# Taps given out by counted work, and parts of VectorE's work moved to ScalarE and a DMA, in a hybrid attention and convolution layer

## The chip, the cores and the metric

The kernel runs on one core of one Trainium2 chip. The metric is the device time of one execution in microseconds (us). Before the change it is 491.62 us, the median of 3 runs (489.23 to 491.92). The engines are named as the profile names them: PE (TensorE, matmul), PEld (its weight loads), DVE (VectorE), ACT (ScalarE), POOL (GpSimd) and SP (SyncE, which issues all DMAs of the kernel before).

## The reference, cut to what matters

One encoder layer for 1024 prompt frames and 64 sample frames, with 16 meta tokens, 1104 tokens in all, of 1024 features in f32. One input projection feeds an attention group and a convolution group; each is normalised, gated and multiplied with its half of the output projection.

```python
q, k, v, ga, u, gb = _split(_rms(h_p, g_pre[l]) @ w_in[l])      # u = a * sigmoid(b)
att  = _prompt_attention(q, k, v, mk, mv, sinks[l])             # windows of 3 chunks of 64 keys + meta
conv = _conv_branch(u, left, conv_w[l], ln_g[l], ln_b[l], w_pw[l])
#   31 depthwise taps over u, LayerNorm over channels, silu, @ w_pw
y = concat([_rms(att, g_att) * silu(ga), _rms(conv, g_conv) * silu(gb)]) @ w_out
h_p = h_p + _rms(y, g_post)
```

The softmax is over the keys and a learned sink; its P is e / sum, and P multiplies v.

## The kernel before, in words

**Products in three parts.** A product of f32 accuracy is three products of rounded parts: high weights x high x, high weights x low x, low weights x high x. `hi_w` (L162) copies a raw weight tile of 128 x 1024 into its high part, mostly on ACT; `lo_w` (L174) subtracts that from the raw tile on DVE. `split_w` is both. A unit (`unit`, L301) is one weight tile times one of three token groups n (384, 384, and 336 or 320 columns): 8 k-slices x 3 parts = 24 matmuls. In the first group (n = 0) it takes all 16 matmuls with high weights first (`SK`), in the others slice by slice (`KS`). At a fixed point of a unit (`ahead`, L179) the weights of the next one are split: for the GLU's `a` weights (AT) at n = 0, for its `b` weights (BT) at n = 2, else at n = 1. `load_raw` puts the weight after that on SP's queue; the raw tiles have two buffers. `WORDER` (L44) is the order of the weights: AT, BT, AT+1, BT+1, KM (keys), AT+2, BT+2, VM (values), AT+3, BT+3, the four q tiles (QT), the gates, and two tiles of the pointwise weights.

**The start** (L681 to L765). x comes in three token groups. Group 0 is split without its norm; the norm's factor goes into the results of the first four units (`late`). Later `renorm` (L261) scales the tile of group 0 on DVE, and `resplit` (L266) splits it again on ACT and DVE. Groups 1 and 2 are squared row by row on ACT (`square_rows`), the sums become a factor (`stat_x`, DVE and POOL), which `diag_x` (DVE) and `bcast_x` (a matmul) spread, `scale_x` (DVE) multiplies, and `hi_x`, `lo_x` split. Lists `at={step: [...]}` say behind which matmul each such step is issued. a0, b0, a1, b1 are the units of the first two pairs of GLU weights; a0[0] and b0[0] are their units on group 0, run in turn, matmul by matmul.

**Order.** Instructions stay in program order on each engine (`keep_in_program_order`), so the place where the Python code issues something is its place in the queue.

**Taps.** When the GLU output u of one of four channel groups is complete, `conv` (L422) puts 31 taps into the list `taps`; each is one DVE instruction over 1118 columns of H. Behind every matmul of a unit, `tick` (L331) may issue one: it counts matmuls, and whenever the count reaches `pace` (9.2, 9.4, 10.0 or 7.5 in different parts), the next tap goes out.

**Attention** (L881 to L932). `order` has 17 chunks of 64 queries. One pass of the loop issues the scores of chunk i (`att_scores`: 12 matmuls, then a bias and a minimum on DVE into T), the high and low parts of the next queries (`att_prep`: ACT, DVE), the transposes of the chunk before (`att_transpose`; PSUM copies on ACT, in later chunks one of two on DVE), the exponentials of chunk i (ACT), their division by the sums (`norm`, L618: a reciprocal and four scalings on DVE), and the products with v of the chunk before (`att_values`). Between these, `fill` issues matmuls of the 24 gate units' queue. From pass L0 = 11 on, the taps that are left are issued at once, and the LayerNorm runs in steps (`ln_pre`, `ln_mean`, `ln_var`, `ln_diag`, `ln_scale`). Pass 17 also splits the last pointwise weights. Then come the pointwise products and the output projection.

Of the kernel before, what the change touches and what calls it, by code (L numbers as in the profile page):

```python
# [48 lines left out]
def layer_kernel(ctx: ExitStack, tc: tile.TileContext, x, x_fm, w_in, w_pw, w_out, vec, g_post,  # L49
# [13 lines left out]

    class Engine:


        def __init__(self, engine):
            self.engine = engine

        def __getattr__(self, name):  # L70
# [288 lines left out]
    def ab_units(i, seqs=(None,) * 3, bps=(("s", 2),) * 3):  # L359
# [48 lines left out]
        for n in range(3):  # L408
            out.append((unit(AT + i, n, done_a, seqs[n]), unit(BT + i, n, done_b, seqs[n], bps[n])))
# [229 lines left out]
    def att_transpose(c):  # L639
# [3 lines left out]
        for n, (end, v) in enumerate(avs.pop(c)):  # L643
# [4 lines left out]
            if n == 0 or c == NCHUNK or c < 8:  # L648
# [33 lines left out]
    for _ in range(11):  # L682
# [6 lines left out]
    load_raw(1, [h1])  # L689
# [29 lines left out]
    def by(u, m):  # L719
# [5 lines left out]
    HW_, LW = hi_w, lo_w  # L725
    hi_x(0, 0)
    hi_w(0, b=4)
    hi_w(1, True, b=4)
    lo_x(0, 0)
    run(a0[0], b0[0], at={  # L730
        0: [L(S, 0, 1), L(S, 0, 2), L(LW, 0, b=4), L(LW, 1, b=4)],
        6: [L(S, 0, 3), L(S, 0, 4), L(HW_, 0, a=4), L(HW_, 1, True, a=4), L(S, 0, 5)],
        9: [L(S, 0, 6), L(S, 0, 7), L(LW, 0, a=4), L(LW, 1, a=4), L(load_raw, 3, [h1, h2])]
        + [L(load_x, 1, g) for g in range(3)] + [L(load_rows, 0, 0)],
        16: [L(split_w, 2, dst=(wq[:, 0], wq[:, 1]), b=4), L(split_w, 2, a=4)]})
    run(a1[0], at={
        0: [L(Q, 1, 0), L(Q, 1, 1), L(split_w, 3, dst=(wq[:, 2], wq[:, 3]), b=4), L(split_w, 3, a=4), L(Q, 1, 2), L(load_rows, 0, 1, 2)] + [L(load_x, 2, g) for g in range(3)]
        + [L(load_rows, 2, 0)],
        18: [L(stat_x, 1)]})
    run(b1[0], at={  # L740
        0: [L(diag_x, 1)],
        12: [L(bcast_x, 1), L(N, 1, 0)] + [L(H_, 1, k) for k in range(3)],
        18: [L(L_, 1, k) for k in range(3)] + [L(Q, 0, 0), L(load_rows, 2, 1), L(N, 1, 1), L(Q, 0, 1), L(load_rows, 2, 2)]})
# [36 lines left out]
    def add_ab(i):  # L780
        pace[0] = 9.4
# [3 lines left out]
    def add_kv(mi, dst):  # L785
        pace[0] = 9.4
# [84 lines left out]
    pace[0] = 9.4  # L871
# [10 lines left out]
    pace[0] = 10.0  # L882
# [3 lines left out]
    fill(16)  # L886
    L0, GATE, REST = 11, (9, 11, 12, 14, 16), 72
    for i in range(max(len(order) + 1, L0 + 7)):
# [28 lines left out]
        if 0 < i <= len(order):  # L917
            att_values(order[i - 1])
        if 0 < i < len(order):
            att_v(order[i])  # L920
        if i == len(order):
# [254 lines left out]
```

## Time and profile before

| | us |
|---|---|
| time, median of 3 runs | 491.62 (489.23 to 491.92) |
| the profiled execution: its time, its span | 493.84, 492.0 |
| busy PE, PEld, DVE | 468.4, 422.7, 392.6 |
| busy ACT, POOL | 213.6, 83.4 |
| mean granted TensorE clock, as a share of full speed | 0.974 |

The span is from the first to the last instruction. Matmuls are pipelined and their ends are modelled, so a busy PE need not be at its peak; how many matmuls it gets through in a stretch says more. The stretches used below: 0 to 68 us the start, 68 to 196 the remaining units up to q, with taps, 196 to 362 attention with the gate units, then the pointwise products and the output projection. The busy time of an engine is a mean over these stages, and each has its own limit.

### The profile page before, as it was taken

The numbers are of one execution on the slowest core, as the hardware profiler recorded it, in microseconds if no ns is written. First come the engines' busy times: TensorE is split into PE (matmuls) and PEld (weight loads), VectorE is DVE, ScalarE is ACT, GpSimd is POOL, SyncE is SP. The second block draws the span as 40 slices with busy tenths as digits, with TensorE's granted clock in tenths as the row PEclk, the third lists the DMA queues.
The fourth block names the chain that finished last, engine by engine and source line by source line (L and its number), as shares of the span: only waits on it lengthen the run. The fifth ranks groups of instructions, "written<-read, shape, count | busy, mean of one in ns | idle before, by whom it ended". The sixth has DMA issues, their size and how long they took to land.

```text
span 492.0 us, 7351 instructions
## 1 busy us (share of the span) xinstructions
PE 468.4 (95%) x2801; PEld 422.7 (86%) x2801; DVE 392.6 (80%) x684; ACT 213.6 (43%) x500; POOL 83.4 (17%) x105
## 2 busy tenths in 40 slices
PE   7988979999999999899999987999999999999994
PEld 6968979999999999898888875888999887888884
DVE  3565789999999999999999997798587955654533
ACT  5565333024212122356666543656687434433322
POOL 0000100000000000000332133164464521011100
PEclk8999989999999999899999987999999999999998
DMA  8993011101202111110101010102113602322221
GB/s 286 338 357 110 0 29 62 45 30 59 65 5 86 43 44 43 44 43 7 47 7 45 7 47 3 50 24 69 44 52 120 213 27 86 103 85 87 85 106 66
DMA packets 14474, 37.76 MB, mean 77 GB/s; under 512 B 2376, under 2 KB 4664, under 8 KB 14440
## 3 DMA queue, kind: packets, MB, share of 16 engines
q1 hardware_dynamic: 14440, 37.31, 22.6%
q8 instruction: 22, 0.36, 0.3%
q14 instruction: 12, 0.10, 0.1%
HBM read 32.00 MB, written 4.84 MB: 75 GB/s over the span
## 4 chain that ended last, share of the span: by engine, by line
PE 52%; DVE 36%; ACT 4%; issue 3%; DMA 3%; SPq 1%; POOL 0%; DVEq 0%; POOLq 0%; ACTq 0%
PE g L81 23%; DVE H L74 20%; PE y L81 19%; DVE T L74 4%; PE pw L81 4%; ACT xT L74 3%; DVE wlo L74 3%; DVE xT L74 2%; DMA H<-in_x_dram 2%; PE s L81 2%; PE av L81 1%; DMA x<-in_x_fm_dram 1%; DVE x L74 1%; DVE qs L74 1%; DVE wo L74 1%
## 5 line engine op out<-in xcount | busy, mean ns | idle before, releaser
L81 PE MATMUL g<-xT,whi 128*128 128x384 f32 (+2 forms) x960 | 231.8, 341 | 4.1 <-ACT whi L74 2.7
L81 PEld LDWEIGHTS g<-xT,whi 128*128 128x128 f32 x960 | 171.1, 193 | 12.4 <-ACT whi L74 2.9
L74 DVE SCALAR_TENSOR_TENSOR H<-u,vec_t,H 128x1118 f32<-128x1118 f32 x120 | 166.6, 1388 | 2.5
L81 PE MATMUL g<-xT,wlo 128*128 128x384 f32 (+2 forms) x480 | 138.1, 334 | 0.0
L81 PEld LDWEIGHTS g<-xT,wlo 128*128 128x128 f32 x480 | 89.4, 190 | 2.2 <-issue 1.5
L81 PE MATMUL y<-wo,mh 128*128 128x512 f32 (+2 forms) x304 | 89.1, 381 | 0.2 <-DVE wo L74 0.2
L81 PEld LDWEIGHTS y<-wo,mh 128*128 128x128 f32 (+1 forms) x304 | 55.1, 185 | 12.1 <-DVE wo L74 0.6
L81 PE MATMUL y<-wo,ml 128*128 128x512 f32 (+1 forms) x136 | 51.2, 378 | 0.0
L74 POOL TENSOR_TENSOR asq<-asq 128x128 f32<-128x128 f32 (+2 forms) x18 | 17.4, 964 | 124.2 <-ACT asq L74 123.5
L74 DVE SCALAR_TENSOR_TENSOR y<-y,small,y 128x512 f32<-128x512 f32 (+1 forms) x19 | 13.7, 720 | 28.2 <-PE y L81 28.2
L74 ACT ACTIVATE T<-T,st 128x210 f32<-128x210 f32 (+2 forms) x68 | 30.4, 451 | 9.6 <-DVE st L74 9.6
L81 PEld LDWEIGHTS y<-wo,ml 128*128 128x128 f32 x136 | 25.6, 188 | 4.5
L74 ACT ACTIVATE yj<-y 128x512 f32<-128x512 f32 (+2 forms) x21 | 12.8, 608 | 30.7 <-DVE y L74 30.6
L74 DVE TENSOR_TENSOR wlo<-wraw,whi 128x1024 fp32r<-128x1024 f32 (+1 forms) x23 | 25.8, 1130 | 0.0
L81 PE MATMUL g<-xT,wq 128*128 128x384 f32 (+1 forms) x144 | 25.4, 333 | 0.0
L81 PEld LDWEIGHTS g<-xT,wq 128*128 128x128 f32 x144 | 24.2, 188 | 0.5
L74 ACT ACTIVATE whi<-wraw 128x1024 fp32r<-128x1024 f32 (+1 forms) x21 | 21.2, 1011 | 6.5 <-PE g L81 6.1
L74 ACT ACTIVATE PT<-pa 128x512 f32<-128x512 f32 (+2 forms) x17 | 10.1, 596 | 28.4 <-PE pa L84 28.4
L74 DVE CUSTOM_DVE_ANT_0 T<-s,bias 128x210 f32<-128x210 f32 (+2 forms) x68 | 20.6, 358 | 1.8 <-PE s L81 1.8
L74 ACT ACTIVATE qb<-g 128x384 f32<-128x384 f32 (+1 forms) x12 | 5.7, 475 | 36.5 <-PE g L81 36.5
L74 POOL MEMSET gb<- 128x30 f32 x4 | 1.6, 391 | 110.2 <-PE g L81 60.5
L74 ACT ACTIVATE y<-y,small 128x512 f32<-128x512 f32 (+1 forms) x19 | 12.6, 665 | 15.3 <-PE y L81 15.3
(195 smaller groups left out, 604.3 us busy)
## 6 DMA issues: line engine op xcount, KB each, us to landing
wraw<-in_w_in_dram SPq DMA_DIRECT2D x18, 512.0 KB, 3.4
H<-in_x_dram SPq DMA_DIRECT2D x8, 512.0 KB, 7.2
xr<-in_x_dram SPq DMA_DIRECT2D x8, 512.0 KB, 4.1
out_dram<-o SPq DMA_DIRECT2D x7, 512.0 KB, 2.9
woraw<-in_w_out_dram SPq DMA_DIRECT2D x6, 512.0 KB, 3.5
wraw<-in_w_in_dram SPq DMA_DIRECT2D x8, 256.0 KB, 5.5
x<-in_x_fm_dram SPq DMA_DIRECT2D x4, 384.0 KB, 6.3
x<-in_x_fm_dram SPq DMA_DIRECT2D x2, 576.0 KB, 6.9
```

What stands on the lines that cost most here:

```text
L74: ins = op(*a, **k)
L81: return tc.keep_in_program_order(nc.tensor.matmul(*a, **k))
```

## The change

It keeps a count of planned time per engine, `given`, in nanoseconds: each matmul adds its columns at 2.4 a nanosecond plus 14, at least 109 (half for 64 rows); each operation of ACT adds 200 + 0.82 per column, of DVE 60 + 1.18 per column, from PE's count on if that is further. `tick` issues taps while DVE's count is less than 600 ns ahead of PE's. `freer` answers "act" or "dve" and decides at three places. For weights from the fifth on, `lo_w` may copy the negated high part on ACT and have a DMA from POOL's queue add the raw weights to it. P's scalings may go to ACT, one by one. P's PSUM copies go to either. The products with v move from the end of a pass to behind the scores of the next one, and there is one pass more. The LayerNorm's first pass L0 is now found in the loop: from pass 9, when fewer than 2 taps are left, or pass 12. In the start, a0[0] runs alone and then b0[0], with b0's raw weights loaded behind x; `renorm` moves from the last part of the start to b1[1]'s matmuls; the split for KM moves one unit ahead.

```diff
+    given = dict(pe=0.0, dve=0.0, act=0.0)
...
                 ins = op(*a, **k)
+                if self.name:
+                    n = columns(k["out"] if "out" in k else a[0])
+                    given[self.name] = max(given[self.name], given["pe"]) + self.each * (1 + ("accum_out" in k)) + self.column * n
                 return keep(ins) if pinned[0] else ins
...
+    act, dve, pool = Engine(nc.scalar, "act", 200, 0.82), Engine(nc.vector, "dve", 60, 1.18), Engine(nc.gpsimd)
+    def freer():
+        return "act" if given["act"] < (given["pe"] + LATE if taps else given["dve"]) else "dve"
+    def mm(out, lhsT, rhs, **k):
+        n = columns(rhs) * (4 if rhs.dtype == F32 else 1) / 2.4
+        if lhsT.shape[0] == HD or out.shape[0] == HD:
+            n /= 2
+        given["pe"] += max(14 + n, 55 if lhsT.shape[0] == HD else 109)
+        return tc.keep_in_program_order(nc.tensor.matmul(out, lhsT=lhsT, rhs=rhs, **k))
...
     def lo_w(p, a=0, b=KT):
...
+        if p > 3 and freer() == "act":
+            act.activation(lo, hi.bitcast(F32), AF.Copy, scale=-1.0)
+            pool.dma_start(out=lo, in_=raw, accum_op=ALU.add)
+            return
         dve.tensor_tensor(out=lo, in0=raw, in1=hi.bitcast(F32), op=ALU.subtract)
...
+    FIRST = [(0, 0), (0, 1), (1, 0), (1, 1), (0, 2), (1, 2)] + [(k, s) for k in range(2, KT) for s in (0, 2, 1)]
+    SECOND = [(k, s) for m in (0, 4) for s in (0, 1, 2) for k in range(m, m + 4)]
...
-    pace = [9.2, 0]
+    AHEAD, LATE = 600, 2500
     def tick():
-        if taps:
-            pace[1] += 1
-            if pace[1] >= pace[0]:
-                pace[1] -= pace[0]
-                f, j = taps.pop(0)
-                f(j)
+        while taps and given["dve"] < given["pe"] + AHEAD:
+            f, j = taps.pop(0)
+            f(j)
...
             for i in range(4):
-                keep(dve.tensor_scalar(out=T[:, i, lo:], in0=T[:, i, lo:],
-                                             scalar1=st[:, 8 + i:9 + i], scalar2=None, op0=ALU.mult))
+                if freer() == "act":
+                    act.activation(T[:, i, lo:], T[:, i, lo:], AF.Copy, scale=st[:, 8 + i:9 + i])
+                else:
+                    dve.tensor_scalar(out=T[:, i, lo:], in0=T[:, i, lo:], scalar1=st[:, 8 + i:9 + i],
+                                      scalar2=None, op0=ALU.mult)
...
-            if n == 0 or c == NCHUNK or c < 8:
+            if freer() == "act":
                 act.activation(pt[:k, n, :], ps[:k, :], AF.Copy)
...
-    load_raw(1, [h1])
...
+    load_raw(1, [h1, h2])
     load_raw(2, [h1, h2])
...
-    run(a0[0], b0[0], at={
...
+    run(a0[0], at={
+        2: [L(S, 0, 2), L(S, 0, 3), L(S, 0, 4)],
+        6: [L(HW_, 0, a=4), L(LW, 0, a=4), L(S, 0, 5), L(S, 0, 6), L(S, 0, 7)],
+        12: [L(HW_, 1, b=4), L(LW, 1, b=4), L(HW_, 1, a=4), L(LW, 1, a=4)]})
+    run(b0[0], at={
...
-    run(b1[1], at={2: [L(Q, 2, 0), L(Q, 2, 1), L(Q, 2, 2)], 8: [L(stat_x, 2)]})
+    run(b1[1], at={0: [L(Q, 2, 1), L(Q, 2, 2)], 4: [L(R, 0), L(R, 1), L(stat_x, 2)], 8: [L(R, 2), L(R, 3)],
+                   16: [L(diag_x, 2), L(R, 4), L(R, 5)]})
...
-        0: [L(renorm, k) for k in range(3)], 2: [L(resplit, 0)] + [L(renorm, k) for k in range(3, 6)],
-        4: [L(resplit, 1)] + [L(renorm, k) for k in range(6, 8)], 6: [L(resplit, 2)]})
-    run(a1[2])
-    run(b1[2], at={0: [L(split_w, 4)]})
+        0: [L(R, 6), L(R, 7)] + [L(resplit, g) for g in range(3)]})
+    run(a1[2], at={0: [L(split_w, 4)]})
+    run(b1[2])
...
-    fill(16)
-    L0, GATE, REST = 11, (9, 11, 12, 14, 16), 72
...
+    fill(24)
+    L0, GATE, REST = 99, (9, 11, 12, 14, 16), 72
+    i = -1
+    while (i := i + 1) < max(len(order) + 2, L0 + 7 if L0 < 99 else 0):
         left = len(order) + 1 - i
+        if L0 == 99 and i >= 9 and (i == 12 or len(taps) < 2):
+            L0 = i
...
             exps, norm = att_scores(order[i])
+        if 2 < i <= len(order) + 1:
+            att_values(order[i - 2])
+        if 1 < i < len(order):
+            att_v(order[i])
```

## Rows read from the trace of the kernel before

**Rows 1.** Busy time by stretch: PE, PEld, DVE, ACT, POOL; clock, DMA, GB/s.
```profile
0.00:68.00 68.00, 59.30 (x317) 55.15 (x317) 40.36 (x79) 34.74 (x61) 6.06 (x20) 0.97 0.57 197
68.00:196.00 128.00, 127.75 (x763) 126.75 (x763) 125.88 (x120) 27.58 (x56) 1.33 (x2) 0.99 0.15 49
...
221.00:271.00 50.00, 49.86 (x366) 41.51 (x365) 48.68 (x121) 32.05 (x101) 12.01 (x13) 1.00 0.08 26
271.00:303.00 32.00, 26.81 (x169) 21.00 (x169) 30.09 (x71) 13.70 (x42) 7.31 (x7) 0.89 0.07 22
```

**Rows 2.** PE's waits in the whole span: us in total, times, longest.
```profile
PE mu L81 <- DVE ga L74: 2.9, 1, 2.9
...
PE s L81 <- DVE qs L74: 2.4, 1, 2.4
PE av L81 <- DVE PT L74: 2.1, 1, 2.1
```

**Rows 3.** The chain that ended last, from 60 to 125 us: start, us, what.
```profile
67.89 5.75 PE g L81 x24
...
80.08 36.12 PE g L81 x216
```

**Rows 4.** Timeline of DVE, ACT and PE in the start: start, us, engine, line, operation.
```profile
56.18 1.67 DVE L74 SCALAR_TENSOR_TENSOR x<-x,vec_t,rbc 128x384 f32<-128x384 f32 x3
59.08 1.36 DVE L74 TENSOR_TENSOR xT<-x,xT 128x1152 fp32r<-128x1152 f32 x1 [1.24 <-ACT xT L74]
...
66.79 1.05 ACT L74 ACTIVATE whi<-wraw 128x1024 fp32r<-128x1024 f32 x1
...
18.32 6.40 PE L81 MATMUL g<-xT,wq 128*128 128x384 f32 x36
...
67.89 4.36 PE L81 MATMUL g<-xT,whi 128*128 128x384 f32 x16 [2.67 <-ACT whi L74]
```

**Rows 5.** Timeline of PE in attention: the scores' matmuls of four chunks.
```profile
221.34 0.90 PE L81 MATMUL s<-kx,qs 64*128 64x146 f32 x12
...
271.33 0.92 PE L81 MATMUL s<-ky,qs 64*128 64x210 f32 x12
...
302.48 1.61 PE L81 MATMUL s<-ky,qs 64*128 64x210 f32 x12
...
312.23 0.92 PE L81 MATMUL s<-ky,qs 64*128 64x210 f32 x12
```

**Rows 6.** DVE by shape, 68 to 196 us: count, busy us, mean ns, idle before.
```profile
L74 DVE SCALAR_TENSOR_TENSOR H<-u,vec_t,H 128x1118 f32<-128x1118 f32 x78 | 107.8, 1382 | 2.1
L74 DVE TENSOR_TENSOR wlo<-wraw,whi 128x1024 fp32r<-128x1024 f32 x11 | 13.4, 1219 | 0.0
L74 DVE TENSOR_SCALAR H<-u,vec_t 128x1118 f32<-128x1118 f32 x3 | 2.4, 801 | 0.0
```

**Rows 7.** ACT: two rows of its timeline, one of its shapes over the span.
```profile
81.97 0.45 ACT L74 ACTIVATE kTb<-g 128x336 f32<-128x336 f32 x1 [1.48 <-PE g L81]
82.32 1.05 ACT L74 ACTIVATE whi<-wraw 128x1024 fp32r<-128x1024 f32 x1
...
L74 ACT ACTIVATE xT<-x,vec_t 128x384 fp32r<-128x384 f32 x16 | 8.8, 606 | 12.8 <-DVE x L74 8.0 <-DMA x<-in_x_fm_dram 4.8
```

**Rows 8.** DMA issues in 68:200, 0:60 and 200:300 us: count, KB each, us to landing.
```profile
wraw<-in_w_in_dram SPq DMA_DIRECT2D x11, 512.0 KB, 3.4
...
wraw<-in_w_in_dram SPq DMA_DIRECT2D x2, 512.0 KB, 7.0
...
vE<-vtok SPq DMA_DIRECT2D x6, 32.0 KB, 1.7
```

**Rows 9.** DVE and ACT by shape, 221 to 271 us.
```profile
L74 DVE SCALAR_TENSOR_TENSOR H<-u,vec_t,H 128x1118 f32<-128x1118 f32 x20 | 28.3, 1416 | 0.2
...
L74 DVE TENSOR_SCALAR T<-T,st 128x210 f32<-128x210 f32 x20 | 5.8, 353 | 0.2
...
L74 ACT ACTIVATE T<-T,st 128x210 f32<-128x210 f32 x24 | 11.0, 461 | 1.8 <-DVE st L74 1.8
```

More of the change, by code (lines that the diff above doesn't have):

```diff
@@ L62, in layer_kernel, with columns, __init__ @@
     pinned = [True]
+    given = dict(pe=0.0, dve=0.0, act=0.0)
+    def columns(ap):
+        n = 1
+        for m in ap.shape[1:]:
+            n *= m
+        return n
     class Engine:
-        def __init__(self, engine):
+        def __init__(self, engine, name=None, each=0, column=0):
             self.engine = engine
+            self.name, self.each, self.column = name, each, column
         def __getattr__(self, name):
@@ L408, in ab_units @@
         for n in range(3):
-            out.append((unit(AT + i, n, done_a, seqs[n]), unit(BT + i, n, done_b, seqs[n], bps[n])))
+            out.append((unit(AT + i, n, done_a, seqs[n]), unit(BT + i, n, done_b, SECOND if seqs[n] is FIRST else seqs[n], bps[n])))
         return out
@@ L724, in layer_kernel @@
     Q = square_rows
-    HW_, LW = hi_w, lo_w
+    HW_, LW, R = hi_w, lo_w, renorm
     hi_x(0, 0)
     hi_w(0, b=4)
-    hi_w(1, True, b=4)
     lo_x(0, 0)
-    run(a0[0], b0[0], at={
-        0: [L(S, 0, 1), L(S, 0, 2), L(LW, 0, b=4), L(LW, 1, b=4)],
-        6: [L(S, 0, 3), L(S, 0, 4), L(HW_, 0, a=4), L(HW_, 1, True, a=4), L(S, 0, 5)],
-        9: [L(S, 0, 6), L(S, 0, 7), L(LW, 0, a=4), L(LW, 1, a=4), L(load_raw, 3, [h1, h2])]
+    hi_x(0, 1)
+    lo_x(0, 1)
+    lo_w(0, b=4)
+    run(a0[0], at={
[3 more added lines that the diff above has]
+    run(b0[0], at={
+        0: [L(split_w, 2, dst=(wq[:, 0], wq[:, 1]), b=4), L(split_w, 2, a=4), L(load_raw, 3, [h1, h2])]
         + [L(load_x, 1, g) for g in range(3)] + [L(load_rows, 0, 0)],
-        16: [L(split_w, 2, dst=(wq[:, 0], wq[:, 1]), b=4), L(split_w, 2, a=4)]})
+        12: [L(Q, 1, 0), L(Q, 1, 1)]})
     run(a1[0], at={
-        0: [L(Q, 1, 0), L(Q, 1, 1), L(split_w, 3, dst=(wq[:, 2], wq[:, 3]), b=4), L(split_w, 3, a=4), L(Q, 1, 2), L(load_rows, 0, 1, 2)] + [L(load_x, 2, g) for g in range(3)]
-        + [L(load_rows, 2, 0)],
-        18: [L(stat_x, 1)]})
+        0: [L(Q, 1, 2), L(load_rows, 0, 1, 2)] + [L(load_x, 2, g) for g in range(3)] + [L(load_rows, 2, 0)],
+        6: [L(split_w, 3, dst=(wq[:, 2], wq[:, 3]), b=4), L(split_w, 3, a=4), L(stat_x, 1)]})
     run(b1[0], at={
         0: [L(diag_x, 1)],
-        12: [L(bcast_x, 1), L(N, 1, 0)] + [L(H_, 1, k) for k in range(3)],
-        18: [L(L_, 1, k) for k in range(3)] + [L(Q, 0, 0), L(load_rows, 2, 1), L(N, 1, 1), L(Q, 0, 1), L(load_rows, 2, 2)]})
+        6: [L(bcast_x, 1), L(N, 1, 0)] + [L(H_, 1, k) for k in range(3)],
+        18: [L(L_, 1, k) for k in range(3)] + [L(Q, 0, 0), L(load_rows, 2, 1), L(N, 1, 1)]})
     load_raw(4)
@@ L885, in layer_kernel @@
     att_v(order[0])
-    fill(16)
-    L0, GATE, REST = 11, (9, 11, 12, 14, 16), 72
-    for i in range(max(len(order) + 1, L0 + 7)):
+    fill(24)
+    L0, GATE, REST = 99, (9, 11, 12, 14, 16), 72
+    i = -1
+    while (i := i + 1) < max(len(order) + 2, L0 + 7 if L0 < 99 else 0):
         left = len(order) + 1 - i
+        if L0 == 99 and i >= 9 and (i == 12 or len(taps) < 2):
+            L0 = i
         quota = (max(24, -(-(len(queue) - REST) // left)) if i else 48) if left > 0 else 26
         n = i - L0
-        if i == 2:
-            pace[0] = 7.5
         if i < len(order):
             exps, norm = att_scores(order[i])
+        if 2 < i <= len(order) + 1:
+            att_values(order[i - 2])
+        if 1 < i < len(order):
+            att_v(order[i])
+        if i == len(order) + 1:
+            split_w(len(WORDER) - 1, on_dve=True, dst=[sm.tile([P, KT, P], F32R, tag=t, bufs=1, name=f"w1{t}")
+                                          for t in ("kT", "vT")])
         if i + 1 < len(order):
@@ L916, in layer_kernel @@
         fill(8 if left > 0 else 4)
[L917 to L921, printed above, removed]
-            split_w(len(WORDER) - 1, on_dve=True, dst=[sm.tile([P, KT, P], F32R, tag=t, bufs=1, name=f"w1{t}")
-                                          for t in ("kT", "vT")])
+        if i == 1:
+            att_values(order[0])
+            att_v(order[1])
         if 3 <= i < len(order) + 3:
```

20 lines of the change are left out of this document (5 added, 15 removed).

## The prediction

> **What bounds the kernel now.** I read the busy times by stretch first, then TensorE's (PE's) waits, then the stretches where they lie. From 68 to 196 us PE is busy 127.8 of 128 us and VectorE (DVE) 125.9: both are full, and PE sets the pace: none of its long waits lies there [rows 1, 2]. Its pace is 216 matmuls in 36.12 us, 0.167 us each [rows 3]. Time that PE could still give back is therefore in three places only.
>
> First, the start. PE works 59.3 of 68 us, and at 67.89 it stands 2.67 us for ACT's `whi`, because that copy is queued behind the last third of the x tile that is scaled and split again; the 24 matmuls after the pause take 5.75 us where 24 x 0.167 = 4.0 is the pace, so the pause costs 2.67 + 1.75 = 4.4 us [rows 3, 4]. Second, the entry of attention: the first scores wait 2.4 us for DVE's `qs` [rows 2]. Third, the last chunks before the taps end. Scores of the 3rd chunk (order number 2) start at 221.34, of number 9 at 271.33, of number 12 at 302.48: (271.33 - 221.34)/7 = 7.14 us a chunk, then 31.15/3 = 10.4 [rows 5]. From 271 to 303 PE works 26.8 of 32 us at a granted clock of 0.89, with DVE at 30.1 [rows 1]; the mean product waits 2.94 us for DVE in there. That is the loop at L0 = 11 which issues all taps left, then the channel sums, ahead of P's scaling.
>
> **The change, part by part.**
>
> *Renorm earlier, KM's split earlier.* Eight `renorm` steps (three take 1.67 us, so eight 4.5) leave the chain that runs from 56.2 to 67.9 [rows 4]; six go beside b1[1]'s matmuls, where DVE is not full (40.4 of 68 us busy [rows 1]). Behind x2's last split, which ends at 56 us, stay two renorms (1.1 us) and the low parts of eight tiles (three take 1.36, so 3.6 us): some 61 us [rows 4]. `split_w(4)` stands one unit earlier too, behind that. PE is through its starting products at 67.89 - 2.67 = 65.2, so nothing is late: -4.4. What is late next is the third broadcast: two renorms stand before its statistics on DVE and could hold PE 1 us more.
>
> *First products singly, b0's weights loaded later.* The same 48 matmuls, the same 14 splits on DVE and ACT, the same bytes ahead of the row loads. One x tile takes 0.6 us on ACT [rows 7] and as much on DVE; DVE has eight of these and two 0.7 us halves of a weight's low part between x's arrival, some 7.5 us, and the end of a0, which comes to 14; b0's 24 matmuls then run without waits (4.0), where both were fed in turn before. Both end at 18 us, as now: a1's first product starts at 18.32 [rows 4]. Moving b0's raw load behind x takes half a MB off x's way; the fourth weight's load waits for the first's low part, which now stands earlier on DVE. Between -2 and +2; I take -0.6. The start: -5.
>
> *Low weight parts by ACT and an adding DMA.* Each takes a 1.22 us subtraction off DVE (11 of them from 68 to 196, 13.4 us [rows 6]) and adds an ACT copy (the high part's twin, 1.05 us [rows 7]) and a 512 KB DMA from POOL's queue, SBUF to SBUF, of which the trace has none. ACT hides the copy (busy 27.6 of 128 us [rows 1]). The DMA's cover is the lead from the split to the first use of the low part. At n = 0 a unit uses high parts for 16 matmuls first. With a split one unit ahead that is 24 + 16 = 40 matmuls x 0.167 = 6.7 us, and this holds at four places: BT+2, VM, BT+3, QT. ACT is held by the copy of the unit before: `kTb` from 81.97, `whi` 82.32 to 83.37 [rows 7]; its negative ends at 84.3, 2.4 us into the lead. So the DMA has 4.3 us. Nearest rows: a 512 KB weight load alone 3.4 us, in the crowded start 7.0, a 32 KB SBUF copy 1.7 [rows 8]. Below: 1.7, no wait. Above: 7.0, 2.7 us late, and with a pause's 1.75 us of slow matmuls 4.45 x 4 = 18 us. I take a little more than the 3.4 us row, since it has the size but does not read its target: half a microsecond late at each, +2. The other places have 64 matmuls, 10.7 us, and wait for nothing up to a landing of 8 us. Behind the issue on POOL stand only statistics that are needed a chunk later, and the raw buffer's next load on SP waits for the DMA instead of DVE: it has a whole unit. For a DMA issued from GpSimd, the Trainium skill (DMA: Bandwidth & Descriptors, Anatomy of one DMA) gives 2.0 us and the bytes at 436 GB/s, 3.2 us here without an addition; by that the four waits would be nothing and the total 2 us better.
>
> The 78 taps of that stretch have two inputs in SBUF and take 1.38 us each; the three opening taps, of one input, take 0.80 at the same size [rows 6]. The Trainium skill (SBUF — State Buffer, Who interferes with whom) has GpSimd locked out of writing DMA descriptors while DVE runs an operation that uses both of its ports, and counts single-input scalings, not two-input ones, among those. By this rule only the 0.80 us taps could delay an issue; if every tap did, each place would come up to 1.4 us later. No run here shows which.
>
> *Taps by counted work.* Before, a tap came after every 9.2 to 10 matmuls (7.5 later); now whenever DVE's count is under 0.6 us ahead of PE's. In the full stretch that alone changes nothing. But the 13.4 us free 13.4/1.4 = 9 to 10 taps' room, and DVE is free 6 us sooner at the start, 4 more. Of the 124 taps, 43 are left at 196 us now; I expect 29 or 30.
>
> *P scaled by ACT while taps remain.* A chunk's four scalings cost DVE 4 x 0.35 = 1.4 us [rows 9]. On ACT they have no row at 210 columns; the exponentials of that size take 0.46 [rows 9], and plain columns with a pointer scale 0.61 at 384 [rows 7], so 0.36 to 0.46 each, 1.5 to 1.8 a chunk. ACT is busy 32.05/7 = 4.6 us a chunk from 221 to 271 [rows 1]: 6.1 to 6.4, with low parts 6.7 of 7.14. It fits, without much room; its counted work is higher than the rows (an exponential counts 0.57), so part goes back to DVE: I count half.
>
> *Attention, summed.* DVE's work besides taps falls from (48.7 - 20 x 1.42)/7 = 2.9 us a chunk to about 2. That leaves 5 us, 3.6 taps a chunk. Thirty taps end at about chunk 8, before L0 = 9 is allowed, so nothing is left to issue at once. Chunks then stay at 7.14: 31.15 - 3 x 7.14 = 9.7, of which 0.7 for the mean's matmul moves only: -9. The slow chunk after (302.48 to 312.23, 9.75, where a chunk with the same steps costs some 9): -0.8. Of the 2.4 us at the entry, eight more matmuls ahead of it (1.3 us) take half: -1.2. Attention -11. At best PE loses nothing more (-17); at worst the freed DVE time is filled with taps up to the count and chunks stay as they are (0).
>
> *v products behind the next scores, one more pass.* The same matmuls, one chunk later; it gives P's copies a chunk more (one such copy held PE for 2.1 us [rows 2]) and adds no work. The 20 matmuls of the added pass come from those kept for the end. 0.
>
> Sum: -5 + 2 - 11 = -14. The profiled span is 492.0 us, its execution 493.84, 2.2 above the runs' median of 491.62. Taken from the median: 477.6, say **478 us**.
>
> **Rivals.** (a) *The adding DMA is late.* An addition reads two operands, and POOL issues it behind ACT. Every microsecond beyond 4.3 stops PE four times, with the slow matmuls after: 4 x (late + 1.75). The 16 us of the rest are used up at 2.25 us late, a landing of 6.6 us. At 9 us: 4 x (4.7 + 1.75) = 26, and 0.8 at each of some six others: 31 - 16 = +15, 507 us, slower. For it: the 7.0 us loads; against: the queue is nearly empty there. (b) *ACT becomes the bound in attention*: PE waits for its copies, and 10 chunks last 8.1 instead of 7.14 us: 478 + 10 = 488. Against: 6.7 of 7.14. (c) *It does not do what it says*: ACT's count runs ahead, DVE keeps scalings and late low parts, and a heap is left at L0 = 12. Half of the 11 goes: 484. (d) *Better*: no DMA wait, the whole 2.4 us and the statistics' waits gone: 471.
>
> **How the numbers follow.** Chances: forecast 0.48, a 0.14, b 0.12, c 0.12, d 0.14. Its own range is 473 to 482. The range of 467 to 492 leaves out most of (a) and a little of (d). Half a per cent, 2.5 us, is what a measurement can tell. Faster: forecast, d, 0.11 of c, 0.06 of b, 0.79. The same: 0.04 each of a and b, 0.01 of c, 0.09. Slower: 0.10 of a and 0.02 of b, 0.12.
>
> **What would show it.** Right: no PE pause near 65 us and KM's first product before 64; 9 or 10 more taps before the first scores; chunks 9 to 12 at 7 to 7.5 us; no DVE heap ahead of the first mean. Wrong: PE pauses for `wlo` between 80 and 145 us, a landing above 6 us, chunks above 8 us with ACT full, or a third broadcast so late that the start gains nothing.

## The result, and the profile after

The changed kernel takes 489.24 us (median of 20 runs), the kernel before, beside it, 492.23: a ratio of 0.9917, 95% interval 0.9888 to 0.9946. Three microseconds are gained where 14 were forecast. Here and below, medians are over all runs, and ratios leave out the runs that are over 1.5% above the fastest of their kernel. The profiled execution took 490.5 us, span 488.7 (before 493.84 and 492.0). The table goes by landmarks of PE's timeline in these two executions, and in one of the two fastest versions of the experiments (c2, below). The first convolution output is the transpose `uo` right behind KM's first unit; number 12 is an order number, as in [rows 5]; pointwise products are those named `pw`.

| us | before | changed | difference | forecast | c2 |
|---|---|---|---|---|---|
| to the first convolution output | 73.48 | 72.52 | -1.0 | -5 | 65.88 |
| from there to the scores of number 12 | 229.00 | 218.67 | -10.3 | -8.2 | 217.78 |
| from there to the first pointwise product | 59.91 | 63.73 | +3.8 | -0.8 | 60.46 |
| from there to the end | 129.61 | 133.78 | +4.2 | 0 | 132.38 |
| span | 492.0 | 488.7 | -3.3 | -14 | 476.5 |

1.7 us of c2's start is a drop (below) at 10 us that the other two executions had. The middle gained 2 us more than forecast. The start gained little, and 8 us were given back behind number 12. Busy time by stretch, changed kernel (columns as in [rows 1]):

```profile
0.00:68.00 68.00, 60.79 (x314) 58.14 (x315) 43.54 (x81) 36.38 (x63) 5.17 (x15) 0.92 0.57 203
68.00:196.00 128.00, 126.45 (x762) 124.84 (x761) 123.13 (x114) 38.48 (x66) 11.44 (x17) 1.00 0.38 91
...
221.00:271.00 50.00, 50.00 (x377) 43.19 (x376) 44.77 (x122) 34.35 (x108) 9.71 (x11) 1.00 0.09 28
271.00:303.00 32.00, 30.19 (x212) 25.18 (x210) 24.66 (x65) 19.85 (x61) 8.71 (x11) 0.95 0.11 34
303.00:362.00 59.00, 55.99 (x370) 48.51 (x369) 44.04 (x105) 37.91 (x92) 25.26 (x30) 0.97 0.17 49
```

Against [rows 1], DVE has room from 221 us on, and PE does 212 matmuls from 271 to 303 where it did 169. But the first row has a clock of 0.92 (0.97 before). PE's waits in the changed kernel (us, times, longest; [rows 2]):

```profile
PE xr L104 <- DVE xd L86: 4.5, 2, 2.6
PE rstd L104 <- DVE ra5t L86: 2.2, 1, 2.2
PE mu L104 <- DVE sqc L86: 1.8, 1, 1.8
PE y L104 <- DVE wo L86: 1.5, 2, 0.8
...
PE g L104 <- DMA wlo<-wraw: 1.3, 3, 0.5
...
PE pw L104 <- DVE zh L86: 0.6, 1, 0.6
```

The waits of before for `whi`, `qs` and `PT` are gone. In their place stand longer waits for the broadcasts (3.2 us before), for `rstd` (none) and for the output weights (0.2). So PE is idle for 22.05 us of its span, 23.6 before. Behind such a wait PE often runs part of its next work at the lower of its two clock levels, 1.2 GHz. The two broadcasts of the start, in PE's timeline before, then in that of the changed kernel with KM's first product, and in two windows of the changed kernel:

```profile
36.81 0.91 PE L81 MATMUL xr<-xd,ones_m 128*128 128x384 f32 x2 [1.78 <-DVE xd L74]
...
45.78 0.80 PE L81 MATMUL xr<-xd,ones_m 128*128 128x336 f32 x2 [1.46 <-DVE xd L74]
```

```profile
36.45 0.91 PE L104 MATMUL xr<-xd,ones_m 128*128 128x384 f32 x2 [2.56 <-DVE xd L86]
...
47.44 1.37 PE L104 MATMUL xr<-xd,ones_m 128*128 128x336 f32 x2 [1.92 <-DVE xd L86]
...
68.33 1.40 PE L104 MATMUL g<-xT,whi 128*128 128x384 f32 x7
```

```profile
36.00:42.00 6.00, 5.55 (x21) 5.28 (x22) 2.37 (x7) 3.30 (x7) 0.00 (x0) 0.72 0.49 158
47.00:53.00 6.00, 5.56 (x22) 5.14 (x23) 4.80 (x9) 1.50 (x3) 0.00 (x0) 0.72 0.02 4
```

A granted clock of 0.72 over 6 us is 6 x 0.28 = 1.7 us of work lost; by single microseconds it is 0.50 from 38 to 40 us. I call this a drop. In the kernel before, the clock stayed at 1.00 behind both waits. The last row of the timeline has no wait: KM's pause of [rows 4] is gone, as forecast, and yet KM starts at 68.33 instead of 67.89. How much the start gains varies with the drops: in the executions profiled of e3, e5 and e7 (below), which leave the start as it is, no drop stands behind the third broadcast, and the first convolution output comes at 70.4 to 70.6 us.

In windows of 1 us, the profiled execution before has six drops ahead of its end (at 9, 67, 200 and 289 us, and two from 299), the changed kernel's has six as well (at 10, 37, 47, 289, 327 and 388), c2's none.

Scores in attention [rows 5], and the added rows for low parts [rows 6, 8]:

```profile
219.26 0.89 PE L104 MATMUL s<-kx,qs 64*128 64x146 f32 x12
...
266.68 0.93 PE L104 MATMUL s<-ky,qs 64*128 64x210 f32 x12
...
291.19 1.61 PE L104 MATMUL s<-ky,qs 64*128 64x210 f32 x12
...
299.92 0.92 PE L104 MATMUL s<-ky,qs 64*128 64x210 f32 x12
```

```profile
wlo<-wraw POOLq DMA_DIRECT2D x10, 512.0 KB, 4.5
```

```profile
L86 DVE SCALAR_TENSOR_TENSOR H<-u,vec_t,H 128x1118 f32<-128x1118 f32 x85 | 117.5, 1383 | 2.7
```

From number 2 to 9 it is 47.4 us instead of 50.0, from number 9 to 12 24.5 instead of 31.15 (8.2 a chunk; 7 to 7.5 was the forecast's sign of being right). The adding DMA lands in 4.5 us. 85 long taps stand from 68 to 196, where 78 stood. At the first scores 33 taps are left (44 before), and the last ones run until 281.9 us, in the pass of number 11.

The pass of the 16th chunk is where most of the first 4 us behind number 12 comes back. Before, PE was busy through that whole stretch (59.91 of 59.91 us); now it idles 2.96 us of 63.73. DVE, then ACT and PE in the pass:

```profile
323.09 0.56 DVE L86 SCALAR_TENSOR_TENSOR ga<-ga,g 128x384 f32<-128x384 f32 x1 [2.17 <-ACT ga L86]
324.04 1.23 DVE L86 TENSOR_TENSOR wlo<-wraw,whi 128x1024 fp32r<-128x1024 f32 x1 [0.39 <-ACT whi L86]
325.18 0.67 DVE L86 TENSOR_SCALAR sqc<-ident,rln 128x128 f32<-128x128 f32 x3
...
325.98 1.05 DVE L86 TENSOR_SCALAR T<-T,st 128x210 f32<-128x210 f32 x4
326.94 0.15 DVE L86 TENSOR_SCALAR ra5t<-ra 128x1 f32<-128x1 f32 x1
...
322.13 0.46 ACT L86 ACTIVATE T<-T,st 128x210 f32<-128x210 f32 x1
322.50 0.19 ACT L86 ACTIVATION_READ_ACCUMULATOR T<-T,st 128x1 f32 x1
322.59 0.47 ACT L86 ACTIVATE ga<-g 128x384 f32<-128x384 f32 x1
322.96 1.05 ACT L86 ACTIVATE whi<-wraw 128x1024 fp32r<-128x1024 f32 x1
...
327.14 1.40 PE L104 MATMUL rstd<-sqc,ones_m 128*128 128x384 f32 x2 [2.24 <-DVE ra5t L86]
```

The `rstd` product stands 2.24 us until DVE has read the row statistics out of PSUM (`ra5t`), and DVE reads them behind a gate, a low part, a diagonal and four scalings. A drop follows, 1.7 us. The same work of DVE in the kernel before, and its `rstd`:

```profile
332.64 0.67 DVE L74 TENSOR_SCALAR sqc<-ident,rln 128x128 f32<-128x128 f32 x3
...
333.74 1.05 DVE L74 TENSOR_SCALAR T<-T,st 128x210 f32<-128x210 f32 x4
334.70 0.55 DVE L74 SCALAR_TENSOR_TENSOR ga<-ga,g 128x384 f32<-128x384 f32 x1
335.16 1.22 DVE L74 TENSOR_TENSOR wlo<-wraw,whi 128x1024 fp32r<-128x1024 f32 x1
336.30 0.15 DVE L74 TENSOR_SCALAR ra5t<-ra 128x1 f32<-128x1 f32 x1
...
336.82 0.81 PE L81 MATMUL rstd<-sqc,ones_m 128*128 128x384 f32 x2
```

There the diagonal and the scalings stand ahead of the gate and the low part, and nothing waits. In the changed kernel the gate stands first, and DVE idles 2.17 us for ACT's tanh in front of it. The ACT operations ahead of that tanh are the chunk's four exponentials (an accumulator is read behind each), as in the kernel before; the four scalings of this pass are on DVE.

### The profile page after: what moved, and what is told of

Read it like the earlier page. It is cut to its first block, busy times and chain, and to the rows that moved or that the text cites. A ratio compares the mean times of both kernels' runs of the same rounds, so it can differ in the third digit from the quotient of the medians.

```text
span 488.7 us, 7421 instructions
## 1 busy us (share of the span) xinstructions
PE 466.7 (95%) x2801; PEld 422.9 (87%) x2801; DVE 375.7 (77%) x649; ACT 234.8 (48%) x535; POOL 90.5 (19%) x119
## 4 chain that ended last, share of the span: by engine, by line
PE 67%; issue 9%; DVE 6%; ACT 4%; DMA 3%; POOL 1%; DVEq 0%; POOLq 0%; ACTq 0%; SPq 0%
PE g L104 33%; PE y L104 19%; PE pw L104 4%; PE av L104 3%; PE s L104 3%; DMA wlo<-wraw 2%; DVE wlo L86 2%; PE pa L108 1%; ACT T L86 1%; PE pb L108 1%; DVE H L86 1%; ACT whi L86 1%; DMA woraw<-in_w_out_dram 1%; DVE T L86 1%; PE rstd L104 1%
## 5 line engine op out<-in xcount | busy, mean ns | idle before, releaser
L104 PE MATMUL g<-xT,whi 128*128 128x384 f32 (+2 forms) x960 | 227.5, 337 | 1.2 <-ACT xT L86 1.0
L104 PE MATMUL g<-xT,wlo 128*128 128x384 f32 (+2 forms) x480 | 140.7, 336 | 1.4 <-DMA wlo<-wraw 1.3
L104 PE MATMUL y<-wo,mh 128*128 128x512 f32 (+2 forms) x304 | 90.3, 385 | 1.5 <-DVE wo L86 1.5
L86 ACT ACTIVATE T<-T,st 128x210 f32<-128x210 f32 (+2 forms) x84 | 36.6, 449 | 8.8 <-DVE st L86 8.8
L86 POOL DMA_DIRECT2D wlo<-wraw x13 | 11.5, 884 | 153.6 <-ACT wlo L86 153.6
L104 PE MATMUL g<-xT,wq 128*128 128x384 f32 (+1 forms) x144 | 26.8, 345 | 0.0
L104 PEld LDWEIGHTS g<-xT,wq 128*128 128x128 f32 x144 | 25.5, 197 | 0.7 <-issue 0.4
L86 ACT ACTIVATE sg<-g 128x384 f32<-128x384 f32 (+1 forms) x10 | 4.8, 476 | 36.7 <-PE g L104 36.7
L86 DVE TENSOR_TENSOR wlo<-wraw,whi 128x1024 fp32r<-128x1024 f32 (+1 forms) x10 | 14.5, 1458 | 5.8 <-ACT whi L86 5.8
L86 ACT ACTIVATE qb<-av 128x256 f32<-128x256 f32 x17 | 6.5, 381 | 25.7 <-PE av L104 25.7
```

The source lines that it names most:

```text
L104: return tc.keep_in_program_order(nc.tensor.matmul(out, lhsT=lhsT, rhs=rhs, **k))
```

## The experiments

My theory: the forecast gain is there, and is given back at pauses of PE behind DVE that the change made longer or uncovered (the start's broadcasts, `rstd`, the output weights), each with a drop behind it. Rivals for each place stand in the expectations. Each kernel is the changed one with the edit shown, shortened. Times are medians, ratios those to the kernel before, run beside it; the changed kernel is at 489.24, 0.9917 [0.9888, 0.9946]. The intervals of e1, e2 and e5 overlap with that one, so for each of them by itself the trace decides, and the total only agrees.

**e1_busy_wait**

```diff
 def bcast_x(n):
+    for _ in range({0: 10, 2: 8}.get(n, 0)):
+        matmul(ps[:, :P], lhsT=ident, rhs=ident, start=True, stop=True)
```

> Changed kernel plus 10 and 8 dummy 128x128 products of the identity ahead of the first tile's (xr0) and third tile's (xr2) broadcast product, into the PSUM bank that the broadcast then overwrites; nothing else. After both waits (2.56 us at 36.45, 1.92 us at 47.44) the granted clock was 0.72 and 0.75 for 6 us. Theory (the start's lost gain is the waits and the slow clock behind them): the waits stay as long, but with PE busy through them the clock stays at 1.00; the first convolution output, 72.52 in the changed kernel, comes 2.5 to 3 us earlier (the 22 products behind xr2 took 5.56 us, 4.25 at the pace before; the 21 behind xr0 3.9, 2.4 before), total -2.8 us. Rival (the clock is not it, the products behind the wait are late for their operands): no more than 0.7 us.

486.23 us, 0.988 [0.9839, 0.9922]. First convolution output at 70.22 (72.52), and both windows that had 0.72 have 1.00. The 2.3 us lie a little under the 2.5 to 3 of the theory, and far above the 0.7 of its rival: the drops cost about what the windows say.

**e2_bcast_first**

```diff
-4: [L(L_, 1, 6), L(diag_x, 0), L(L_, 1, 7)],  6: [L(bcast_x, 0), L(Q, 2, 0)]
+4: [L(diag_x, 0), L(L_, 1, 6), L(L_, 1, 7)],  6: [L(Q, 2, 0), L(bcast_x, 0)]
-4: [L(R, 0), L(R, 1), L(stat_x, 2)], ... 16: [L(diag_x, 2), L(R, 4), L(R, 5)]
+4: [L(stat_x, 2), L(R, 0), L(R, 1), L(diag_x, 2)], ... 16: [L(R, 4), L(R, 5)]
```

> Changed kernel with the two broadcasts' statistics ahead of what stands before them: the first tile's diagonal ahead of the low part of x1's 7th block; the third tile's first square sum ahead of the first broadcast's copy on ACT, its statistics ahead of two renorms and its diagonal ahead of the next two. Theory (renorms and low parts in front of the diagonals make PE wait): xr0's wait falls from 2.56 to about 1.4 us, xr2's from 1.92 to 0.8; total -2 us, up to -4 if the clock then stays up. Rival (ACT's square sums set xr2, not the renorms): xr2 moves by under 0.4 us; total -1 us at most.

486.35 us, 0.9871 [0.9836, 0.9905]. PE's timeline:

```profile
33.42 0.91 PE L104 MATMUL xr<-xd,ones_m 128*128 128x384 f32 x2 [1.44 <-DVE xd L86]
...
41.98 0.80 PE L104 MATMUL xr<-xd,ones_m 128*128 128x336 f32 x2 [1.05 <-DVE xd L86]
```

Waits of 1.44 and 1.05 (theory: 1.4 and 0.8), and no drop behind either in this execution; the mean clocks of the ten go from 0.971 to 0.994, so not each was like it. What stood ahead of the diagonals was the cause. For the first broadcast that was DVE's work; for the third the edit moves one of ACT's square sums as well, and which of the two counted was not tested apart.

**e3_norm_rule**

```diff
-return "act" if given["act"] < (given["pe"] + LATE if taps else given["dve"]) else "dve"
+return "act" if given["act"] < given["pe"] + LATE else "dve"
```

> Changed kernel, where the rule that gives a task to ACT or DVE is the one with the allowance of 2.5 us behind PE to the end, and not a comparison of ACT's count with DVE's once no taps remain. Theory (in the pass with the 16th chunk four P scalings and a low part on DVE stand ahead of the row statistics while ACT idles 4.6 us): the 2.24 us wait of PE for rstd at 327 goes, with the slow products behind it, -3.5 us by the start of the pointwise products (354.92 in the changed kernel). Rival (ACT is then late itself, with copies for the score and value products queued behind the scalings): that start moves by less than 1 us, or later, with PE waits for ACT in its place.

488.76 us, 0.9938 [0.9911, 0.9966]. A miss: `rstd` still waits 2.24 us and the first pointwise product stands at 354.54 (354.92). The four scalings stayed on DVE under this rule too (1.05 us at 326.20). The choice between the two rules was not the cause; what stood on DVE ahead of `ra5t` was left to test.

**e5_stats_first**

```diff
+if 3 <= i < len(order) + 3: ... att_stats(c // 2)      # moved up
 for step, at in ((ln_pre, (0,1,3)), (ln_diag, (2, 4, 6))): ...
 if i < len(order): norm()
-if 3 <= i < len(order) + 3: ... att_stats(c // 2)
```

> Changed kernel with the row statistics of a query tile (the product ra and DVE's ra5t) issued ahead of the diagonal of the channel statistics and of P's scaling, instead of behind both; nothing else. In the pass of the 16th chunk the product rstd waited 2.24 us until DVE had read ra5t, which stood behind a low weight part, the diagonal (0.67) and four scalings with their reciprocal (1.2). Theory (the order on DVE is what PE waits for): that wait falls by 1.2 to 1.9 us, and with it the clock's drop of 1.7 us in some runs; total -1 to -3. Rival (the low part behind ACT's tanh and weight copy, itself behind four scalings on ACT, is what is late): the wait stays above 1.5 us and the total within 0.5 us.

485.85 us, 0.9869 [0.9838, 0.9901]. DVE and PE in the same pass:

```profile
323.42 1.22 DVE L86 TENSOR_TENSOR wlo<-wraw,whi 128x1024 fp32r<-128x1024 f32 x1 [0.39 <-ACT whi L86]
324.56 0.15 DVE L86 TENSOR_SCALAR ra5t<-ra 128x1 f32<-128x1 f32 x1
...
325.44 0.88 PE L104 MATMUL rstd<-sqc,ones_m 128*128 128x384 f32 x2 [1.16 <-DVE st L86]
```

The wait falls to 1.16 us and no drop follows in this execution. The order on DVE was the cause of the half that went; what remains is the gate and the low part behind ACT. The "four scalings on ACT" of the expectation are the exponentials named above.

**e4_gate_late** and **e7_no_gate**: the tail.

```diff
# e4: five of the last seven gate products behind the second pointwise tile
-gate_att(order)                        # ahead of gb_silu, and of drain()
+later = gas[2:]; del gas[2:]           # behind drain()
 ...
+if (n, m) == (0, 1): gas.extend(later); gate_att(order)
# e7: none at all
+def gate_att(ready): pass
```

> Changed kernel, where five of the last seven gate products (POOL, two inputs in SBUF) are issued behind the second pointwise tile instead of ahead of the first; they ran from 348.35 to 353.12 beside DVE's subtraction of the pointwise weight's low part, which took 5.73 us (1.22 elsewhere) and stood ahead of zh and zl. Theory (POOL's products hold DVE's subtraction up): it takes at most 2.5 us, zh ends 3 us earlier, the first pointwise evacuation (359.09) comes 2.5 to 4 us earlier, total -2 to -4. Rival (the chain of output weights, loads of 4.4 us and a copy each, sets the tail anyway): subtraction short, total within 1 us. Second rival: the subtraction stays over 4 us, and POOL is not the cause.

> Changed kernel without the attention gate's products on POOL (the gated values are left ungated, 12 products of two SBUF inputs missing); everything else as it is. Theory 1 (the tail gives back 4 us because POOL's products hold up DVE's chain of zh, zl and the output weights): the subtraction of the pointwise weight falls from 5.73 to 1.3 us, the output weights' last low part (386.77, 31.85 behind the first pointwise product) comes 3 to 4 us earlier relative to it, total -3 to -4. Theory 2 (that chain is ACT, DVE and the loads in turn, and POOL only shifts it): subtraction short, but the last low part still 30.5 to 32 us behind the first pointwise product, total within 1.5 us.

491.21 us, 0.9917 [0.9881, 0.9954], and, without the gate's products, 489.17 us, 0.9923 [0.9887, 0.9959]. DVE's subtraction of the pointwise weight, in the changed kernel, in e4 and, with what follows, in e7:

```profile
348.49 5.73 DVE L86 TENSOR_TENSOR wlo<-wraw,whi 128x1024 fp32r<-128x1024 f32 x1 [0.39 <-ACT whi L86]
```

```profile
345.85 2.96 DVE L86 TENSOR_TENSOR wlo<-wraw,whi 128x1024 fp32r<-128x1024 f32 x1 [0.39 <-ACT whi L86]
```

```profile
350.63 1.23 DVE L86 TENSOR_TENSOR wlo<-wraw,whi 128x1024 fp32r<-128x1024 f32 x1 [0.40 <-ACT whi L86]
354.11 0.74 DVE L86 CAST zh<-H 128x1120 fp32r<-128x1120 f32 x1 [2.25 <-ACT H L86]
```

POOL's products do hold it up: 5.73 us beside five of them, 2.96 beside two, 1.23 beside none. The Trainium skill (SBUF — State Buffer, Who interferes with whom) has a DVE operation with two SBUF inputs contend with a GpSimd operation that reads SBUF; these rows agree. But the total does not move clear of noise. Without them `zh` waits for ACT instead, and the last output weight still comes 31.87 us behind the first pointwise product (31.85). I had taken the most striking row for the cause, and the rival was right.

**u1_low_on_dve** and **u5_paced_taps**: one part undone at a time.

```diff
# u1
-if p > 3 and freer() == "act":          # lo_w: negative copy, adding DMA
+if False:
-if L0 == 99 and i >= 9 and (i == 12 or len(taps) < 2):
+if L0 == 99 and i >= 9 and (i == 11 or len(taps) < 2):
# u5: tick as before, pace 9.2, 9.4, 10.0, 7.5
-while taps and given["dve"] < given["pe"] + AHEAD:
+if taps: pace[1] += 1; if pace[1] >= pace[0]: ...
```

> Changed kernel with every low weight part subtracted on DVE again (no adding DMA); the taps left are issued in the pass numbered 11 at the latest, as in the changed kernel. Theory (the room on DVE paid for the faster chunks 9 to 12): some 9 more taps are left at the first scores, the scores of number 12 come 6 to 9 us later (291.19 in the changed kernel), the total 3 to 6 us later. Rival (the adding DMA only moves work about, and costs its own 1.3 us of waits): scores of number 12 within 2 us, total the same or 1 us shorter.

> Changed kernel with the convolution taps given out by counted matmuls again, at the rates of before (one per 9.2 to 10, then 7.5), the rest as changed. Theory (the adding DMA makes the room on DVE, the count is what fills it): some 43 taps left at the first scores as before, instead of 35; a heap is left at pass 11 or 12 of 5 to 8 taps, PE waits 6 to 10 us for the mean there, total +4 to +8. Rival (the rate does not matter, as I costed it at nothing in the full stretch): scores of number 12 within 2 us of 291.19, total within 1.5 us.

498.86 us, 1.0136 [1.0097, 1.0175], and 498.02 us, 1.0114 [1.0071, 1.0157]. Either alone undone makes the kernel slower than before. u1's DVE and PE in pass 11:

```profile
283.10 14.14 DVE L86 SCALAR_TENSOR_TENSOR H<-u,vec_t,H 128x1118 f32<-128x1118 f32 x10
...
298.96 1.65 PE L104 MATMUL mu<-sqc,ones_m 128*128 128x384 f32 x2 [16.16 <-DVE sqc L86]
```

Counted work keeps taps back while DVE is full. Without the room that the DMA makes, ten are left for pass 11, and PE stands 16 us; number 12 comes at 301.18. (u1 also issues what is left in pass 11 at the latest, and not 12.) Paced taps leave 40 for attention (33 in the changed kernel, from the first scores to 310 us) and reach number 12 at 297.28; the mean waits 3.5 us there, not the 6 to 10 that I expected. So undoing either part costs 9.6 and 8.8 us, and each is worth that only beside the other. Both are more than I expected.

**u2_norm_on_dve** and **u3_av_own_pass**

```diff
# u2, norm()
-if freer() == "act":  act.activation(T, T, AF.Copy, scale=...)
+if False:
# u3
-if 2 < i <= len(order) + 1: att_values(order[i - 2])     # behind the next scores
+if 0 < i <= len(order): att_values(order[i - 1])         # end of the pass
```

> Changed kernel with all scalings of P on DVE, as before. Theory (P's scaling by ACT frees 1.4 us of DVE a chunk while taps remain, and only costs something behind the taps): scores of number 12 come 3 to 6 us later; the 2.24 us wait for rstd in the pass of the 16th chunk becomes 1 us or less, since ACT's tanh and weight copy are no longer behind four scalings; total +1 to +3. Rival (what it frees is filled by taps that would have had room anyway): scores of number 12 within 1 us, total -1 to -3.

> Changed kernel with a chunk's v products back at the end of the pass of its transposes, not behind the next scores. Theory (the move gives P's copies a chunk more and no work): PE waits for PT as before (2.1 us once), total 0 to +3. Rival (the later v products hold up the query square sums and with them the statistics; ACT idle for av 15 us from 196 to 291): that idle time falls under 8 us and the total is 1 to 3 us shorter.

487.71 us, 0.9923 [0.9895, 0.9952], and 488.04 us, 0.9922 [0.9888, 0.9955]: no difference that can be measured. In u2 `rstd` waits no more, but the first mean comes in pass 12 instead of 11 and waits 3.7 us for DVE's `st`: the LayerNorm's steps, and with them the pause, moved to other passes, so that u2 is no test of what stood on ACT ahead of the tanh. In u3 no wait for `PT` came back; ACT's idle time for `av` falls from 15.0 to 1.2 us, as its rival has it, and the total still does not tell. Neither theory nor rival gets its number, and no worth of these two parts can be measured here.

**u4_old_start** and **u7_old_start_km**

```diff
# u4: loads, product order and lists of the start as before
# u7: u4, and KM's low part on DVE
-if p > 3 and freer() == "act":
+if p > 4 and freer() == "act":
```

> Changed kernel with the loads, the product order and the lists of the start as before (first two units in turn, renorms behind x2's last split, the fifth weight's split a unit later). Theory (what the new start gains at 65 us it loses at the first and third broadcast): first convolution output within 1.5 us of the 72.52 of the changed kernel apart from clock drops of 1.7 us each, total 0 to +1.5. Rival (the new start is worth the 5 us that I forecast, and only this profile had bad luck with the clock): total +3 to +5.

> Changed kernel with the old start, as u4_old_start, but with the fifth weight's low part (KM, split a unit later in the old start) subtracted on DVE, so that no adding DMA follows so closely on its use: there PE waited 3.0 us for it. Theory (the new start by itself is worth 1 to 3 us, what u4_old_start lost beyond it was that DMA): total 2 to 3.5 us shorter than u4_old_start, 0 to +2 against the changed kernel. Rival (the new start is worth the 4 to 5 us by itself): total within 1 us of u4_old_start.

493.4 us, 1.0038 [1.0014, 1.0062], and 488.03 us, 0.9892 [0.9855, 0.9929]. u4's wait for KM's low part:

```profile
72.53 2.93 PE L104 MATMUL g<-xT,wlo 128*128 128x384 f32 x8 [3.02 <-DMA wlo<-wraw]
```

u4's total fits its rival (+3 to +5), but u7, with the same old start, is no slower than the changed kernel: what u4 lost more was at this DMA. So no worth of the new start by itself can be measured; it is needed where the DMA needs the earlier split. (In u4 and u7, as in u2, the first mean comes a pass later, so they differ from the changed kernel in more than the start.) The 3.02 us are what rival (a) of the prediction would have cost at a place with too little cover.

**c1_start_stats, c2_mean_later, c3_plan**: what the rest points to.

```diff
# c1 = e2 + e5 + five dummy products ahead of each of the two broadcasts
# c2 = c1, and
-fill(2); step((n - d) // 2)
+fill(10 if n == 0 or (n, d) == (4, 2) else 2); step((n - d) // 2)
-fill(... - (2 if 0 <= n <= 6 else 0))
+fill(... - (10 if n in (0, 4) else 2 if 0 <= n <= 6 else 0))
# c3 = c2, and the order of the tail's tasks
-"... h4,z3,M0,l3,h5 . . r0,n0 l4,l5 h6,h7 l6 l7 r1,M1,n1"
+"... h4,z3,M0,l3,h5 l4 l5 r0,n0,h6 h7,l6 l7 . . r1,M1,n1"
```

> Changed kernel with three edits at once: the first and third broadcast's statistics ahead of what stood before them, 5 dummy products ahead of each of these two broadcasts, and the query tiles' statistics ahead of the diagonal and P's scaling. Theory: the gains add, first convolution output at 66 to 68 (72.52 in the changed kernel), pass of the 16th chunk 1 to 2 us shorter, total -5 to -6 against the changed kernel and -8 to -9 against the one before (484). Rival (what is gained ahead is given back by the chain of output weights in the tail): first pointwise product 4 to 6 us earlier, total only -3.

> The three edits of c1_start_stats, and eight queued products more ahead of the first mean's product (pass 11) and of the second rstd's (pass 15), taken from the end of the same passes. Theory (PE only arrives early at both; other products of the queue cover the wait): the 1.9 us wait for the first mean falls under 0.7, the 1.2 us for rstd under 0.3, and the scores of number 12 come 1 to 1.5 us earlier relative to the first convolution output; total -2 against c1_start_stats (479). Rival (DVE is what sets the pace there; the products moved ahead leave a wait at the end of the pass, for T or the next statistics): total within 0.7 us of c1_start_stats.

> As c2_mean_later, and in the pointwise stretch the last four output weights' splits stand up to three tiles earlier in the order (two slots that were empty are used). Theory (the tail's 1.5 us of waits for the output weights, with 1.7 us of slow clock behind in some runs, comes from the order of ACT's and DVE's work): the waits of y for wo fall under 0.5 us, y's first product stays where it is relative to the first pointwise product (26.05), total -1.5 against c2_mean_later. Rival (the chain of loads, ACT and DVE is full, and earlier splits only hold up the evacuations): y's first product comes later by 0.5 us or more, total the same or longer.

481.09 us, 0.9785 [0.9752, 0.9818]; 479.0, 0.9727 [0.97, 0.9753]; 478.81, 0.9726 [0.9702, 0.975]. The gains add, and the intervals of all three lie below that of the changed kernel. In c1 the first convolution output comes at 66.93, inside the 66 to 68 expected. c2's waits:

```profile
PE pw L104 <- DVE zh L86: 2.0, 1, 2.0
...
PE rstd L104 <- DVE H L86: 0.5, 1, 0.5
PE mu L104 <- DVE sqc L86: 0.5, 1, 0.5
...
PE xr L104 <- DVE xd L86: 0.4, 1, 0.4
```

The waits for the mean and `rstd` are short now, but `zh` waits 2.0 us where it waited 0.6: part of the gain moved there. In c3 PE no longer waits for `wo`, but its first output product comes 26.86 us behind the first pointwise one (26.57 in c2, 26.03 in the changed kernel, 25.37 in the one before), and the total is the same. Against c2 that is 0.3 us and not the rival's 0.5, so the rival has the total but only part of the shift. What would shorten the tail was not found.

## Why the prediction was wrong

**The adding DMA (+2): right. Attention (-11): the sum came, but not its parts.** PE waited 1.3 us for low parts where I took 2. The landing of 4.5 us lies close to the row I chose (3.4, "a little more"). The estimate from the Trainium skill (DMA: Bandwidth & Descriptors, Anatomy of one DMA), 3.2 us without an addition, is 1.3 us too short for this DMA, which adds. By landmarks the stretch up to number 12 gained 10.3, 8.2 forecast. Numbers 9 to 12 gave 6.6 of it where I had 9, because the taps lasted to pass 11 and not to chunk 8: 33 were left, not 29 or 30, and the mean still waited 1.8 us. Numbers 2 to 9, costed at nothing ("chunks then stay at 7.14"), gave 2.6: 6.8 us a chunk. That the two make up for each other was luck. Of the 10.3, 4.6 is idle time (from 8.0 to 3.4 us), and some 4 more are drops that the kernel before had behind its waits.

**"In the full stretch that alone changes nothing" (counted taps): wrong by its neighbour.** I costed the counting at nothing by itself. u1 and u5 show that it and the DMA are one part in two pieces.

**The start (-5): failed.** KM's pause went, with its slow products. The step that failed is "what is late next is the third broadcast ... and could hold PE 1 us more": named, but left out of the sum, and with no drop. The first broadcast was not named at all. In the trace the two broadcasts waited 1.24 us longer together (0.78 of it at the first), and a drop of 1.7 stood behind each: 4.6 of the 5. e1 and e2 show both halves. The premise "where DVE is not full (40.4 of 68 us busy)" was a mean over the whole start: from 47 to 53 us DVE was busy 4.8 of 6.

**The sum itself: failed behind number 12.** I carried -11 from number 12 to the end as if nothing there could be late. Two things were. In the pass of the 16th chunk the gate and the low part now stand ahead of the diagonal and the scalings on DVE; DVE idles 2.17 us for ACT's tanh behind the exponentials, and then has everything at once ahead of `ra5t`: 2.24 + 1.7. e5 takes 1.1 us of the wait and the drop back by order alone. Which edit moved the gate forward was not tested. And PE reaches the output products before the weights do: waits of 1.5 (0.2 before) and a drop of 1.7 in the profiled run, and some 0.7 ahead of them. The waits or the time ahead of them stay in every version, c2's tail is 2.8 us longer than before without a drop ahead of its end, and the cause of this part stays open.

**"P scaled by ACT ... I count half" and "v products: 0".** No worth of the first can be measured (u2), nor of the second (u3). 14 of the 48 scalings from 196 to 291 us ran on ACT, not half.

With the pauses covered, c2 is 13.3 us faster than before. That is close to the forecast's 14, but it does not confirm it: c2 has edits that the forecast did not have, the kernel before waits at some of the same places (the broadcasts, the mean) and was not run with these edits, and of the 15.5 us between the two spans some 10 are the six drops that c2 does not have. What I did not do was to ask, at each of PE's next waits on the path, what a faster PE or another order on DVE would make of it.

## What to carry to other kernels

When a stretch gets shorter, go on along the path and list each product that waits for another engine, what is queued ahead of its releaser, and what a drop behind it costs, since the gain is paid out only if none of these is late. Two edits that feed each other (room on an engine, and the rule that fills it) are costed together. A row that is nearly five times its usual length is not a cause until the work behind it is shown to wait for it.

## What the runs showed of the hardware

The runs of one kernel are longer where their mean granted clock is lower. Over its 20 runs the changed kernel's goes from 0.971 (span 489.2) to 0.994 (span 481.6); that the number of drops makes this difference is argued from the traces, which show one run each. Whether a wait is followed by a drop varies: the third broadcast's wait of 1.9 us was followed by one in the trace of the changed kernel, and not in that of e5. In c2's four runs, with the pauses covered, the clock is 0.991 to 0.997.

POOL's issue of an adding DMA took 0.86 to 1.06 us (13 of them), and its landing 4.5 to 5.4 us. The first took 1.06; the other 12 took 0.86 or 0.87, 11 of them beside taps with two inputs and one (at 200.05 us) beside none. So these taps delayed no issue, one half of what the prediction left open. The other half shows at the first issue. In 12 of the traces an opening tap, of one input, starts 0.4 us behind it: the issue takes 1.40 or 1.41 us, and the tap 0.90 to 0.92 instead of 0.80. In the changed kernel, u4 and u7 no such tap starts while it runs, and it takes 1.05 or 1.06. So a one-input tap does hold up an issue, by some 0.35 us there, far less than the 1.4 that the prediction allowed for.
